# Partial products of a Strassen-like projection stay in SBUF while 13 common tiles are free

## The chip, the cores and the metric

The kernel runs on one NeuronCore of one Trainium2 chip. The metric is the device time of one execution in microseconds (us), given as a median over runs. A difference of less than about 0.3% (5 us) counts here as no difference.

## What is computed

The reference is one layer of a streaming encoder. One input projection of the 1024 x 2048 input feeds two mixers side by side: a sparse attention (group A) and a state-space mixer (group B). Their outputs are joined, projected again and normalised. Cut to what matters here:

```python
u = einsum('bsd,de->bse', h, w_in)               # 1024 x 2048 times 2048 x 6752
q, k, v, z_attn, q_idx, k_idx, w_idx, z_ssd, xbc, dt_raw = split(u)
o_attn = dsa_attention(rope(q), rope(k), v, q_idx, k_idx, w_idx) * silu(z_attn)
o_ssd  = ssd_mixer(xbc, z_ssd, dt_raw, ...)      # conv, chunked scan, gated RMSNorm
sub = einsum('bse,ed->bsd', concat(o_attn, o_ssd), w_out)
out = layer_norm(alpha * h + sub)
```

In the sparse attention an indexer scores the keys of each query and only the 256 best are attended; finding the threshold is a search in many short rounds on VectorE and ScalarE. The change touches only how the input projection holds its intermediate sums.

## The kernel before, in words

**Matmul arithmetic.** All big products are float32-accurate. Each operand is split into a high part (`wh`, `xh`, written by ScalarE) and a rest (`wl`, `xl`, written by VectorE or GpSimd), and three matmuls `wh*xh`, `wh*xl`, `wl*xh` make one product of a 128 x 128 block and a 128 x 512 block. One piece of the stream is a column tile of 128 outputs over 8 such blocks: 24 matmuls into one PSUM bank (`pj`, four of them).

**Two groups of pairs.** Most column tiles of the input projection are taken in pairs (`PLAN`, lines 54 to 62; group 0 has 8 pairs, group 1 has 14). Each pair and both halves of the sequence form a 2 x 2 block product that is made with seven products in place of eight (`product`, line 686). The seven lie in four phases (`ph`), with two products (`f` 0 and 1) in the first three phases and one in the last. The pairs of a group are taken two at a time, a couple: in a phase the order is first pair f=0, second pair f=0, first pair f=1, second pair f=1. Products f=0 and f=1 of a pair share one PSUM bank: f=1 goes on adding to what f=0 left, so that before f=1 starts, another engine must have read the bank (event `ev_after`, waited for in `emit_t`, line 1186).

**Intermediate sums.** In phase 0 `t_save` (line 722) copies the first product of a pair with ScalarE into a tile `x` of tag `u`, writes it to DRAM as `P1`, and frees the tile. In phase 1 `t_ld` (line 756) loads `P1` again, and `t_u` (line 734) adds it to the bank on VectorE: after f=0 that is `U2`, after f=1 `U3`; both are written to DRAM and freed. Phases 2 and 3 load `U3`, `U2` and `U3` once more, and `t_comb` (line 763) adds or subtracts the bank on VectorE to make final columns. So a pair writes three tiles of 128 x 512 float32 (256 KB) and reads four; for 22 pairs that is 66 tiles written. In the profile `P1` is named `p`, and `U2` and `U3` are both named `u`, as the SBUF tiles are.

**What sets the order.** There is no order written by hand. The program keeps a list of tasks (Python generators) and a model of the engines' clocks (`Sim`, line 134). `pump` (line 486) looks through the tasks by priority before each quarter of a piece and issues the first one that `ready` (line 438) passes: its events must be due by the model's clock, no engine that it needs may run ahead of TensorE by more than `SLACK` (2650 ns by the model, line 361), and enough tiles must be free (`avail`, line 395, counts them; `keep` holds some back). The weights of a piece are split (`w_split`, line 944) up to `WAHEAD` = 2 pieces ahead of their use. Each engine then executes its instructions strictly in the order in which they were issued. All data transfers go through one queue, SP's. There are 29 tiles of tag `u` (`NU`, line 30); nearly everything that is not an operand of a matmul lives in them.

All engine instructions are issued through one helper, so the profile puts nearly all of them on line 312, and tile names must be read instead: `pj`, `a` and `o` are PSUM banks, `xr` and `s` raw input tiles and attention scores, `wr` raw weights, `wt` and `t` weights in DRAM, `sm` small vectors of the search for the threshold, `cv` the padded tile that the convolution reads.

Of the kernel before, what the change touches and what calls it, by code (L numbers as in the profile page):

```python
# [27 lines left out]
HIDE = -1.0e30  # L28

NU = 29  # L30
N4 = 8
WAHEAD = 2
SKEEP = 4
# [323 lines left out]
class Flow:  # L357

    SLACK = 2650.0
    MARGIN = 300.0

    def __init__(self, nc):
# [73 lines left out]
    def ready(self, task):  # L438
# [13 lines left out]
        for tag, k in n.slots.items():  # L452
            if self.avail(tag) < k + (min(n.keep, self.spare_u) if tag == "u" else 0):
                return False
        slack = self.SLACK * (0.5 if task.prio >= 6 else 2 if task.prio == 0 else 1)
        return all(self.clk[e] <= self.t + slack for e in (n.eng or ("D" if task.prio >= 6 else "")) if e != "P")
# [126 lines left out]
class Layer:  # L583
    def __init__(self, ctx, tc, a):
# [6 lines left out]
        self.dram = pool("dram", bufs=1, space=bass.MemoryType.DRAM)  # L591
        for tag, n in (("xh", 16), ("xl", 16), ("xr", 2), ("wr", 6), ("wh", 3), ("wl", 3), ("u", NU), ("s4", N4), ("cv", 2), ("sm", 6)):
            fl.add_tag(tag, pool("p_" + tag, bufs=1), n)
# [128 lines left out]
    def t_save(self, gi, c, ps):  # L722

        fl = self.fl
        yield Need("A", u=1)
        x = fl.new("u", [P, HALF])
        fl.act(x, ps)
        fl.signal(self.ev_after(gi, c, 0))
        yield Need("")
        fl.dma(self.p_scr("P1", gi, c), x)  # L730
        fl.free(x)
        fl.signal(self.ev_save["P1", gi, c])

    def t_u(self, gi, c, f, ps):

        fl = self.fl
        name = ("U2", "U3")[f]
        yield Need("V", ev=(self.ev_ld[gi, c, 1, 0],), **({} if f else {"u": 1}))
        y = self.ld[gi, c, 1, 0]
        x = y if f else fl.new("u", [P, HALF])  # L740
        fl.tt("V", x, ps, y, ALU.add)
        if f:
            fl.free(ps)
        else:
            fl.signal(self.ev_after(gi, c, 1))
        yield Need("")
        fl.dma(self.p_scr(name, gi, c), x)
        fl.free(x)
        fl.signal(self.ev_save[name, gi, c])

    def pre_ld(self, gi, c, ph, f):
# [3 lines left out]

    def t_ld(self, name, gi, c, ph, f, e):
        fl = self.fl
        yield Need("", u=1, keep=2, ev=(self.ev_save[name, gi, c],))
        x = self.ld[gi, c, ph, f] = fl.new("u", [P, HALF])
        fl.dma(x, self.p_scr(name, gi, c))  # L760
        fl.signal(e)
# [313 lines left out]
    def run(self):  # L1075
        fl = self.fl
        self.ev_save = {(x, g, c): Event() for x in ("P1", "U2", "U3") for g in range(len(GROUPS)) for c in range(len(GROUPS[g]))}
        self.ev_ld, self.ld, self.wacc, self.xst = {}, {}, set(), {}
        self.stream, work = self.units()
        n = len(self.stream)  # L1080
        self.ev_xs = {k: Event() for k in range(8, 4 * len(self.sets))}
        self.ev_xf = [Event() for _ in range(4)]
        self.xf = {(x, kp): self.scratch(f"xf{x}{kp}", [P, 2, HALF]) for x in ("S1", "M3", "M2", "S4") for kp in range(4)}
        self.wraw, self.w, self.ev_wraw = {}, {}, {}
        self.raws, self.passing = {}, set()
        self.warm_up()
        nf = len(FIRST)
        self.nld = self.start(nf)
        for i, rows in work[2 * nf:]:
            p = self.stream[i]  # L1090
            for q in range(4 if p.kind == "T" else len(rows)):
                fl.pump()
                if q == 0:
                    for f in self.hooks.pop(i, ()):
                        f()
                    while self.nsp < n and self.nsp <= i + WAHEAD + (SKEW if self.late(self.nsp) else 0) and self.w_room() and self.w_there(self.nsp, i):
                        self.w_split(self.nsp)
                        self.nsp += 1
                while self.nld < n and self.nld <= i + WAHEAD + 6 and (self.w_more(self.nld) or self.nld <= i + WAHEAD + 1 and self.w_can(self.nld)):
                    self.w_load(self.nld)  # L1100
                    self.nld += 1
                self.need_w(i)
                if p.kind == "T":
                    self.need_x(("t", p.n, 2 * q), ("t", p.n, 2 * q + 1))
                    self.emit_t(i, q)
                else:
                    if q == 0:
                        self.o_tasks(p.h, p.t, p.u)
                    self.need_x((p.h, 2 * p.u), (p.h, 2 * p.u + 1))
                    self.emit_o(i, p.h, p.t, rows, p.u, q)  # L1110
                    if p.t == 1 and q == len(rows) - 1 and p.h < 6:
                        for k in (2 * p.u, 2 * p.u + 1):
                            fl.free(*self.st.pop((p.h, k)))
            if p.kind == "T" or i < n - SKEW or rows[-1] == 3:
                fl.free(*self.w.pop(i))
                fl.settle(fl.t)
        fl.drain()
# [97 lines left out]
    def o_tasks(self, n, d, j):  # L1215
# [5 lines left out]
        if (n, d, j) == (4, 1, 0):  # L1221
            fl.spare = N4
        if (d, j) == (0, 0) and n < 6:
# [1133 lines left out]
```

## Time and profile before

| what | value |
|---|---|
| median of 3 runs | 1664.8 us (1663.27 to 1667.5) |
| the profiled execution | 1667.98 us |
| its span, first to last instruction | 1666.1 us |
| TensorE (PE) busy | 1620.1 us, 97% of the span |
| VectorE (DVE) busy | 1321.7 us, 79% |
| ScalarE (ACT) busy | 1002.0 us, 60% |
| GpSimd (POOL) busy | 197.3 us, 12% |
| moved by DMA | 414.48 MB, mean 249 GB/s |
| mean granted TensorE clock | 0.992 |

In the profile a row such as `PE pj <- DVE u: 5.6, 4, 4.9` means that TensorE sat idle for 5.6 us in all, 4 times, 4.9 us at the longest, until a VectorE instruction writing a tile `u` released it. A timeline row has the start, the duration, the engine and line, the operation, out<-in, the shapes, the count of merged instructions, and in brackets the idle time of the engine just before and who ended it. A windows row has the stretch, its length, the busy time of PE, PEld (weight loads), DVE, ACT and POOL with the number of instructions, then the granted clock as a share of full speed, the busy share of the DMA engines, and GB/s.

### The profile page before, as it was taken

To read this page: it belongs to the slowest core of one execution; us is meant where nothing else is said; L and a number is where in the kernel's file an instruction comes from. 1 tells how busy PE (TensorE), PEld (TensorE's weight loads), DVE (VectorE), ACT (ScalarE), POOL (GpSimd) and SP (SyncE) were. 2 spreads that over 40 slices of the span, in tenths; PEclk is the share of its full clock that TensorE was granted. 3 is DMA by queue.
4 is the path that set the end of the run, shared out by engine and by line. 5 is a ranking of instruction groups with operands and counts; after the bars stand their busy time and mean duration, and the time that the engine had idled before them with its cause. 6 is when DMAs were issued, how large, how long until landed. Compare 5 with 4: busy or idle time off the path is not lost. (4 is left out here: it accounts for less than half of the span.)

```text
span 1666.1 us, 23979 instructions
## 1 busy us (share of the span) xinstructions
PE 1620.1 (97%) x7996; PEld 1340.9 (80%) x7996; DVE 1321.7 (79%) x2429; ACT 1002.0 (60%) x1770; POOL 197.3 (12%) x215
## 2 busy tenths in 40 slices
PE   9999999999998989999999999999999999999997
PEld 7787777888787768888888888888877888888885
DVE  5889998997778866788676669875787687659998
ACT  4555666779787788776344456776866555532330
POOL 0100010000000000122212202222010000100110
PEclk9999999999999999999999999999999999999999
DMA  8177574789768856687786584656988889668664
GB/s 309 52 280 258 189 262 168 268 303 334 290 230 324 294 196 234 235 304 277 260 288 218 180 286 161 210 171 210 334 284 307 316 300 325 215 232 274 220 202 152
DMA packets 192387, 414.48 MB, mean 249 GB/s; under 512 B 19720, under 2 KB 55688, under 8 KB 192264
## 3 DMA queue, kind: packets, MB, share of 16 engines
q1 hardware_dynamic: 191832, 412.56, 71.7%
q8 instruction: 63, 1.03, 0.2%
q14 instruction: 60, 0.49, 0.1%
q10 hardware_dynamic: 432, 0.39, 0.1%
HBM read 308.94 MB, written 103.94 MB: 248 GB/s over the span
## 5 line engine op out<-in xcount | busy, mean ns | idle before, releaser
L312 PE MATMUL pj<-xh,wh 128*128 128x512 f32 (+1 forms) x1496 | 585.7, 392 | 14.5 <-ACT u L312 6.0
L312 PE MATMUL pj<-xh,wl 128*128 128x512 f32 (+1 forms) x1496 | 573.6, 383 | 5.1 <-DVE wl L312 5.1
L312 PE MATMUL pj<-xl,wh 128*128 128x512 f32 (+1 forms) x1496 | 573.0, 383 | 0.0
L312 DVE TENSOR_TENSOR wl<-wr,wh 128x1024 fp32r<-128x1024 f32 (+2 forms) x236 | 282.4, 1201 | 172.4 <-ACT wh L312 170.4
L312 PEld LDWEIGHTS pj<-xh,wh 128*128 128x128 f32 x1496 | 283.8, 190 | 68.6 <-issue 7.5
L312 PEld LDWEIGHTS pj<-xh,wl 128*128 128x128 f32 x1496 | 283.5, 190 | 63.1 <-DVE wl L312 7.3
L312 PEld LDWEIGHTS pj<-xl,wh 128*128 128x128 f32 x1496 | 284.0, 190 | 49.1
L312 ACT ACTIVATE wh<-wr 128x1024 fp32r<-128x1024 f32 (+2 forms) x242 | 248.1, 1031 | 120.0 <-PE pj L312 82.8
L312 PE MATMUL a<-u,u 128*128 128x512 f32 (+3 forms) x736 | 172.8, 354 | 7.6 <-DVE s L312 4.4
L312 PEld LDWEIGHTS a<-u,u 128*128 128x128 f32 x736 | 120.7, 189 | 42.5 <-DVE s L312 18.6
L312 ACT ACTIVATE u<-a 128x512 fp32r<-128x512 f32 (+4 forms) x115 | 53.2, 479 | 153.3 <-DVE u L312 58.0
L312 ACT ACTIVATE u<-s,sm 128x640 bf16<-128x640 int16 (+7 forms) x132 | 129.7, 983 | 22.1 <-DVE sm L312 20.0
L312 DVE TENSOR_TENSOR u<-u,u 128x512 f32<-128x512 f32 (+6 forms) x204 | 128.6, 645 | 5.7 <-DMA u<-wo 1.3
L312 PE MATMUL pj<-wh,xh 128*128 128x512 f32 x310 | 125.2, 404 | 0.5 <-DVE u L312 0.5
L312 PE MATMUL pj<-wh,xl 128*128 128x512 f32 x310 | 121.0, 390 | 0.0
L312 PE MATMUL pj<-wl,xh 128*128 128x512 f32 x310 | 121.0, 390 | 0.0
L312 ACT ACTIVATE a<-a 128x512 f32<-128x512 f32 (+3 forms) x160 | 77.1, 505 | 68.3 <-PE a L312 65.5
L312 ACT ACTIVATE u<-u 128x512 f32<-128x512 f32 (+4 forms) x146 | 80.1, 558 | 52.4 <-DVE u L312 43.9
L312 DVE TENSOR_TENSOR u<-pj,u 128x512 f32<-128x512 f32 (+2 forms) x112 | 74.7, 668 | 45.7 <-PE pj L312 42.2
L312 DVE TENSOR_TENSOR wr<-wr,wr 128x1024 f32<-128x1024 f32 (+1 forms) x81 | 99.8, 1233 | 0.8 <-DMA wr<-wt 0.4
L312 POOL TENSOR_SCALAR s<-s,sm 128x640 f32<-128x640 f32 (+7 forms) x64 | 63.8, 1011 | 124.0 <-DVE sm L312 97.4
L312 DVE SCALAR_TENSOR_TENSOR u<-cv,cw,u 128x512 f32<-128x512 f32 x96 | 73.0, 766 | 6.7 <-ACT u L312 3.5
(259 smaller groups left out, 2200.3 us busy)
## 6 DMA issues: line engine op xcount, KB each, us to landing
wr<-wt SPq DMA_DIRECT2D x187, 512.0 KB
u<-u SPq DMA_DIRECT2D x110, 256.0 KB
wr<-t SPq DMA_DIRECT2D x44, 512.0 KB
u<-wo SPq DMA_DIRECT2D x64, 256.0 KB
ts<-u SPq DMA_DIRECT2D x64, 256.0 KB
wr<-ts SPq DMA_DIRECT2D x32, 512.0 KB
s<-xt SPq DMA_DIRECT2D x24, 512.0 KB
t<-wr SPq DMA_DIRECT2D x22, 512.0 KB
```

The costliest lines, as they stand in the source:

```text
L312: f(*args, **kw)
```

## The change

Where at least 13 tiles of tag `u` are free at the moment when an intermediate sum is finished, its tile is not freed but kept in a table `kept`. A kept `P1` or `U2` isn't written to DRAM and not loaded; `t_ld` hands the tile on at once. A kept `U3` is still written, since it is needed twice, and only its first load is left out. `t_ld` asks for the save's event first and for a free tile only if it must load. Next to that, `SLACK` goes from 2650 to 2620.

```diff
@@ -28,6 +28,7 @@
 HIDE = -1.0e30
 
 NU = 29
+KEEP_U, KEEP_G = 13, 9
 N4 = 8
 WAHEAD = 2
 SKEEP = 4
@@ -358,7 +359,7 @@
 
 
 
-    SLACK = 2650.0
+    SLACK = 2620.0
     MARGIN = 300.0
 
     def __init__(self, nc):
@@ -727,9 +728,15 @@
         fl.act(x, ps)
         fl.signal(self.ev_after(gi, c, 0))
         yield Need("")
-        fl.dma(self.p_scr("P1", gi, c), x)
-        fl.free(x)
+        if self.may_keep("P1", gi):
+            self.kept["P1", gi, c] = x
+        else:
+            fl.dma(self.p_scr("P1", gi, c), x)
+            fl.free(x)
         fl.signal(self.ev_save["P1", gi, c])
+
+    def may_keep(self, name, gi):
+        return name in ('P1', 'U2', 'U3') and gi < KEEP_G and self.fl.avail("u") >= KEEP_U
 
     def t_u(self, gi, c, f, ps):
 
@@ -744,8 +751,13 @@
         else:
             fl.signal(self.ev_after(gi, c, 1))
         yield Need("")
-        fl.dma(self.p_scr(name, gi, c), x)
-        fl.free(x)
+        stay = self.may_keep(name, gi)
+        if not stay or name == "U3":
+            fl.dma(self.p_scr(name, gi, c), x)
+        if stay:
+            self.kept[name, gi, c] = x
+        else:
+            fl.free(x)
         fl.signal(self.ev_save[name, gi, c])
 
     def pre_ld(self, gi, c, ph, f):
@@ -755,7 +767,12 @@
 
     def t_ld(self, name, gi, c, ph, f, e):
         fl = self.fl
-        yield Need("", u=1, keep=2, ev=(self.ev_save[name, gi, c],))
+        yield Need("", ev=(self.ev_save[name, gi, c],) if (name, gi, c) not in self.kept else ())
+        if (name, gi, c) in self.kept:
+            self.ld[gi, c, ph, f] = self.kept.pop((name, gi, c))
+            fl.signal(e)
+            return
+        yield Need("", u=1, keep=2)
         x = self.ld[gi, c, ph, f] = fl.new("u", [P, HALF])
         fl.dma(x, self.p_scr(name, gi, c))
         fl.signal(e)
@@ -1076,6 +1093,7 @@
         fl = self.fl
         self.ev_save = {(x, g, c): Event() for x in ("P1", "U2", "U3") for g in range(len(GROUPS)) for c in range(len(GROUPS[g]))}
         self.ev_ld, self.ld, self.wacc, self.xst = {}, {}, set(), {}
+        self.kept = {}
         self.stream, work = self.units()
         n = len(self.stream)
         self.ev_xs = {k: Event() for k in range(8, 4 * len(self.sets))}
```

In the built program the condition is met for 10 of the 66 tiles: in group 0 one `P1` (pair 7), four `U2` (pairs 0, 1, 2 and 7) and four `U3` (pairs 1, 5, 6 and 7), in group 1 a single `U3` (pair 8). SP's queue has 1206 DMAs of data where it had 1221, 15 of 256 KB fewer. The matmuls are the same and as many, 7682 instructions in all. ScalarE has 57 table loads in place of 53 and otherwise as many instructions; three sums move from GpSimd to VectorE. The first instruction that is gone is the write of `P1` of pair 7, which stood at 330.99 us in the profile; up to there the orders of all engines are the same, and after it the scheduler takes other decisions on every engine, in the second group and beyond. The last 40 instructions of VectorE, the normalisation, are again the same in kind and order.

Three places show what moved. The first is VectorE in the last phase of group 0, ahead of the split of the weight of pair 3: `wl` is the rest of a weight of the next piece, `wr<-wr,wr` a sum of two raw weights, `cv` and `u<-pj` combine a bank with a loaded or kept sum, `u<-cv,cw` is the convolution. Before (the split of the weight before this one is row 782):

```order
793 L312 SCALAR_TENSOR_TENSOR sm_2975<-sm_2975 128x2
794 L312 TENSOR_TENSOR sm_3784<-sm_3784 128x2
795 L312 TENSOR_SCALAR sm_3784<-sm_3784 128x2
796 L312 SCALAR_TENSOR_TENSOR sm_3784<-sm_3784 128x2
797 L312 SCALAR_TENSOR_TENSOR u_5209<-cv_5356,cw,u_5209 128x512 x3
798 L312 SCALAR_TENSOR_TENSOR u_5094<-cv_5412,cw,u_5094 128x512 x3
799 L312 TENSOR_TENSOR wr_5374<-wr_5374,wr_5375 128x1024
800 L312 TENSOR_TENSOR wl_5432<-wr_5229,wh_5431 128x1024
801 L312 TENSOR_TENSOR wl_5436<-wr_5270,wh_5435 128x1024
```

Now:

```order
790 L313 TENSOR_TENSOR wl_5296<-wr_5093,wh_5295 128x1024
791 L313 TENSOR_TENSOR xl_5320<-xr_5199,xh_5319 128x512
792 L313 TENSOR_TENSOR xl_5324<-s_893_5219,xh_5323 128x512
793 L313 TENSOR_TENSOR xl_5328<-s_893_5219,xh_5327 128x512
794 L313 TENSOR_TENSOR wr_5254<-wr_5254,wr_5255 128x1024
795 L313 TENSOR_TENSOR cv_5347<-pj_5117,u_4333 128x512
796 L313 TENSOR_TENSOR wr_5309<-wr_5309,wr_5310 128x1024
797 L313 TENSOR_TENSOR wl_5351<-wr_5209,wh_5350 128x1024
```

Before, between the two weights (rows 782 and 800) there were two convolutions of three steps each, nine small steps of the search and three sums of weights, and the next weight was split right behind. Now three splits of `x`, two sums of weights and one combination lie between them, and the convolution stands behind the weight.

The second place is ScalarE in phase 0 of group 1, at the second couple (pairs 2 and 3). `u<-pj` is `t_save` of a pair: the bank is free for its second product only when it is done. `u,sm<-` are steps of the search, `wh` is the split of a weight; the table load with the ten instructions on `s` behind it belongs to the state-space mixer. Before:

```order
608 L312 ACTIVATE u_6044<-pj_6006 128x512
609 L312 ACTIVATE u_2976,sm_2975<-s_109_745,sm_2975 128x896
610 L312 ACTIVATE u_2976,sm_2975<-s_110_746,sm_2975 128x1024
611 L312 ACTIVATE wh_6053<-wr_5787 128x1024
612 L312 ACTIVATE u_3785,sm_3784<-u_2425,sm_3784 128x384
613 L312 ACTIVATE u_3785,sm_3784<-u_2426,sm_3784 128x512
614 L312 ACT_TABLE_LOAD
615 L312 ACTIVATE u_5501<-s_953_5496 64x512 x2
616 L312 ACTIVATE s_953_5496<-s_953_5496,ac_241 128x128 x8
617 L312 ACTIVATE u_6107<-pj_6057 128x512
```

Now:

```order
589 L313 ACTIVATE wh_5939<-wr_5668 128x1024
590 L313 ACTIVATE u_5880<-u_5880 128x512
591 L313 ACTIVATE u_2976,sm_2975<-s_109_745,sm_2975 128x896
592 L313 ACTIVATE u_2976,sm_2975<-s_110_746,sm_2975 128x1024
593 L313 ACTIVATE u_5928<-u_5928 128x512
594 L313 ACT_TABLE_LOAD
595 L313 ACTIVATE u_5494<-s_950_5489 64x512 x2
596 L313 ACTIVATE s_950_5489<-s_950_5489,ac_241 128x128 x8
597 L313 ACTIVATE u_5994<-pj_5945 128x512
598 L313 ACTIVATE wh_5998<-wr_5722 128x1024
599 L313 ACTIVATE u_2976,sm_2975<-s_109_745,sm_2975 128x896
600 L313 ACTIVATE u_6035<-pj_6002 128x512
```

Row 608 before was the save of pair 2 and row 617 that of pair 3; now they are rows 597 and 600. The block that begins with the table load stood between the two saves, and stands now ahead of both.

The third place is ScalarE later in phase 0 of group 1, at the couple of pairs 10 and 11, from the split of the weight of pair 11's first product to that of pair 10's second. `s,sm<-s,sm` are exponentials of the attention, `u<-pj` with a table load ahead of it is a SiLU, `u,sm<-u,sm` are steps of the search. Before:

```order
697 L312 ACTIVATE wh_6844<-wr_6557 128x1024
698 L312 ACTIVATE u_3785,sm_3784<-u_2425,sm_3784 128x384
699 L312 ACTIVATE u_3785,sm_3784<-u_2426,sm_3784 128x512
700 L312 ACT_TABLE_LOAD
701 L312 ACTIVATE u_6898<-pj_6694 128x512
702 L312 ACTIVATE u_3785,sm_3784<-u_2425,sm_3784 128x384
703 L312 ACTIVATE u_3785,sm_3784<-u_2426,sm_3784 128x512
704 L312 ACT_TABLE_LOAD
705 L312 ACTIVATE s_1154_6742,sm_6789<-s_1154_6742,sm_6789 128x640
706 L312 ACTIVATE s_1155_6743,sm_6789<-s_1155_6743,sm_6789 128x640
707 L312 ACTIVATE wh_6932<-wr_6576 128x1024
```

Now (the split of the weight before `wh_7013` is row 698, and row 701 is one more table load):

```order
703 L313 ACTIVATE s_1164_6761,sm_6784<-s_1164_6761,sm_6784 128x768
704 L313 ACTIVATE u_3781,sm_3780<-u_2425,sm_3780 128x384
705 L313 ACTIVATE u_3781,sm_3780<-u_2426,sm_3780 128x512
706 L313 ACTIVATE u_6967<-a_6962 128x512
707 L313 ACTIVATE u_3781,sm_3780<-u_2425,sm_3780 128x384
708 L313 ACTIVATE u_3781,sm_3780<-u_2426,sm_3780 128x512
709 L313 ACT_TABLE_LOAD
710 L313 ACTIVATE u_6985<-pj_6684 128x512
711 L313 ACT_TABLE_LOAD
712 L313 ACTIVATE s_1180_6853,sm_6907<-s_1180_6853,sm_6907 128x768
713 L313 ACTIVATE s_1181_6854,sm_6907<-s_1181_6854,sm_6907 128x768
714 L313 ACTIVATE wh_7013<-wr_6577 128x1024
```

Before, the step from one weight to the next had two table loads and two exponentials, in nine instructions between the two splits. Now the step has three table loads and four exponentials, in fifteen: one table load, two exponentials, one pair of search steps and one copy of a bank more.

## The prediction

> **What bounds the kernel now.** I read the busy times first, then the chain that ended last, then who makes TensorE wait, then stretches of the span.
>
> ```profile
> span 1666.1 us, 23979 instructions
> PE 1620.1 (97%) x7996; PEld 1340.9 (80%) x7996; DVE 1321.7 (79%) x2429; ACT 1002.0 (60%) x1770; POOL 197.3 (12%) x215
> 1566.50 21.76 PE pj L312 x96
> ```
>
> TensorE is the bound: 97% of the span, and the last row, from the chain, shows what a dense stretch costs: 96 matmuls in 21.76 us, 0.227 us each, so 5.4 us for a piece of 24. The change removes and adds no matmul. So the time can change only where TensorE idles or runs at a lower clock. These are its longest waits in total:
>
> ```profile
> PE pj L312 <- ACT u L312: 6.0, 2, 4.3
> PE pj L312 <- DVE u L312: 5.6, 4, 4.9
> PE pj L312 <- DVE wl L312: 5.1, 4, 2.6
> PE a L312 <- DVE s L312: 4.4, 7, 2.0
> ```
>
> No row of that answer names a DMA as the releaser of TensorE; the 14 rows name only VectorE, ScalarE and GpSimd. Where do the waits lie? The first two are single events, and stretches of 50 us show the neighbourhood:
>
> ```profile
> 350.00:400.00 50.00, 49.45 (x217) 40.37 (x216) 42.50 (x104) 41.78 (x79) 0.32 (x2) 1.00 0.95 334
> 500.00:550.00 50.00, 43.68 (x186) 35.42 (x186) 43.69 (x78) 38.42 (x71) 3.72 (x7) 0.97 0.85 308
> 550.00:600.00 50.00, 48.27 (x219) 39.37 (x218) 38.63 (x85) 35.90 (x67) 0.80 (x3) 1.00 0.73 260
> 600.00:650.00 50.00, 45.69 (x202) 37.09 (x201) 32.73 (x74) 46.52 (x83) 1.80 (x8) 0.93 0.63 219
> 650.00:700.00 50.00, 50.00 (x229) 41.27 (x227) 38.23 (x89) 37.76 (x70) 3.70 (x4) 1.00 0.77 262
> ```
>
> From 500 to 650 us TensorE is idle for 6.3, 1.7 and 4.3 us. Four waits make nearly all of that:
>
> ```profile
> 519.37 0.77 PE L312 MATMUL pj<-xh,wh 128*128 128x512 f32 x1 [4.89 <-DVE u L312]
> 544.57 0.50 PE L312 MATMUL pj<-xh,wl 128*128 128x512 f32 x1 [1.42 <-DVE wl L312]
> 585.73 0.50 PE L312 MATMUL pj<-xh,wh 128*128 128x512 f32 x1 [1.74 <-ACT u L312]
> 618.56 0.80 PE L312 MATMUL pj<-xh,wh 128*128 128x512 f32 x1 [4.31 <-ACT u L312]
> 519.00:523.00 4.00, 3.63 (x10) 2.96 (x11) 2.67 (x5) 1.32 (x3) 1.23 (x2) 0.60 1.02 388
> 618.00:622.00 4.00, 3.44 (x8) 2.79 (x9) 1.56 (x2) 3.97 (x8) 0.30 (x2) 0.50 0.57 185
> 622.00:626.00 4.00, 4.00 (x14) 3.18 (x13) 3.14 (x4) 3.30 (x7) 0.00 (x0) 0.68 0.68 235
> ```
>
> The three stretches below them show a second price: after the two long waits the granted clock drops. At 0.60 over 4 us TensorE loses 1.6 us, at 0.50 and 0.68 it loses 2.0 and 1.3. So the wait at 519 us costs 6.5 us, that at 618 us 7.6 us.
>
> **The change part by part: the transfers.** Fifteen transfers of 256 KB go, 3.9 MB of 414 MB. What one is to SP's queue:
>
> ```profile
> L312 SPq DMA_DIRECT2D u<-p x22: 320/428/783, 335.7 to 991.5; - x22
> ```
>
> The median issue is 0.43 us, so SP gains about 6 us in all, spread from 331 us to the second group. TensorE waits for no DMA, so I take nothing for them; the cover is that tiles are loaded ahead of their use. The bounds are 0 and, if the stretch at 334 GB/s (the row 350 to 400 above) were bound by transfers, 3.9 MB / 334 GB/s = 11.8 us. That busy row speaks against the upper end: TensorE is busy for 49.45 of its 50 us. The Trainium skill, "DMA: Bandwidth & Descriptors", section Specifications, gives about 358 GB/s as the limit of HBM for one core; by that page the stretch is near its limit, and an estimate from its figure is 11 us of gain. The trace agrees on the rate, and not that the rate binds.
>
> Ten tiles stay held from one phase to the next, out of 29. They are kept only with 13 free, so I take nothing for it; should a task find no tile, it would come later, as part of the next point. `SLACK` is 1% smaller and moves nothing before 331 us.
>
> **The order.** This is what counts: from 331 us the scheduler decides anew. I go through the four waits and put the rows' durations into the new order.
>
> At 544 us TensorE waited for VectorE's split of a weight.
>
> ```profile
> 531.43 1.22 DVE L312 TENSOR_TENSOR wl<-wr,wh 128x1024 fp32r<-128x1024 f32 x1
> 533.17 2.35 DVE L312 TENSOR_TENSOR wr<-wr,wr 128x1024 f32<-128x1024 f32 x2
> 537.68 4.56 DVE L312 SCALAR_TENSOR_TENSOR u<-cv,cw,u 128x512 f32<-128x512 f32 x6
> 542.16 1.22 DVE L312 TENSOR_TENSOR wr<-wr,wr 128x1024 f32<-128x1024 f32 x1
> 543.30 2.35 DVE L312 TENSOR_TENSOR wl<-wr,wh 128x1024 fp32r<-128x1024 f32 x2
> ```
>
> From one split to the next it took 543.30 - 531.43 = 11.9 us, against two pieces of TensorE at 5.4 us. In the new order three splits of `x` at about 0.6 (half of a 1.2 us split, being half as wide), two sums at 1.2, one combination at 0.7 and the split itself make 6.1 us, little more than one piece. The wait goes: -1.4 us. It costs 0 to -1.4.
>
> At 585 us the bank was freed late by ScalarE, by a save that stood behind two steps of the search:
>
> ```profile
> 583.65 0.60 ACT L312 ACTIVATE u<-u,sm 128x384 bf16<-128x384 int16 x1
> 584.38 0.72 ACT L312 ACTIVATE u<-u,sm 128x512 bf16<-128x512 int16 x1
> 585.10 0.57 ACT L312 ACTIVATE u<-pj 128x512 f32<-128x512 f32 x1
> ```
>
> In the new order of ScalarE (rows 571 to 573) the save of pair 0 comes without these two. That is 1.3 of the 1.74 us: -1.3, with bounds 0 and -1.74.
>
> At 519 us the bank of pair 7 waited for a combination on VectorE.
>
> ```profile
> 509.17 1.23 DVE L312 TENSOR_TENSOR wl<-wr,wh 128x1024 fp32r<-128x1024 f32 x1 [4.08 <-ACT wh L312]
> ...
> 518.54 0.68 DVE L312 TENSOR_TENSOR u<-pj,u 128x512 f32<-128x512 f32 x1
> ```
>
> Twelve instructions stand from the first row to the second, 9.4 us. In the new order the tile that this combination adds (`U3` of pair 7) is a kept one, and yet the same twelve, two splits of weights, eight of `x` and two sums, stand ahead of it. So its load was not what made it late, and the wait stays: 0, with bounds of +2 (a part of the 4.08 us idle ahead of it could come twice) and -6.5.
>
> At 618 us ScalarE freed the bank of pair 3 late, after the block of the state-space mixer.
>
> ```profile
> 608.16 1.05 ACT L312 ACTIVATE u<-s,sm 128x896 bf16<-128x896 f32 x1
> 609.33 1.15 ACT L312 ACTIVATE u<-s,sm 128x1024 bf16<-128x1024 f32 x1
> 610.48 1.04 ACT L312 ACTIVATE wh<-wr 128x1024 fp32r<-128x1024 f32 x1
> 612.98 1.28 ACT L312 ACT_TABLE_LOAD   x1
> 615.58 2.44 ACT L312 ACTIVATE s<-s,ac 128x128 f32<-128x128 f32 x8
> 617.93 0.57 ACT L312 ACTIVATE u<-pj 128x512 f32<-128x512 f32 x1
> ```
>
> From the table load to the save it is 617.93 - 612.98 = 4.95 us, about the length of the wait. In the new order this block stands ahead of the save of pair 2, one save earlier. Either pair's second product comes one piece after its first, so the block has the same cover of 5.4 us. I take the wait as moved, not gone: 0, with bounds of +1.9 and -7.6: between the split of the weight and the table load stood 612.98 - 610.48 - 1.04 = 1.5 us, and now stand there the two search steps of the first two rows and two steps of about 0.6, 3.4 us.
>
> **The sum** is -1.4 - 1.3 = -2.7 us against the profiled 1667.98 us, of which the span is 1666.1. Its run lies 3.2 us above the median of the three, so I take the difference over: 1664.8 - 2.7 = 1662.1 us. For the stretches that I didn't go through, mostly behind 650 us, I take nothing: they held few waits before, and may get better or worse. The normalisation at the end is the same.
>
> **The rivals.** *A long wait dissolves.* The waits at 519 and 618 us come from VectorE and ScalarE being late by a few us. For it speaks that VectorE had been idle for 4.08 us just ahead of the twelve instructions, so a split of a weight that ScalarE issues 4 us earlier leaves 0.8 of the 4.89. Against it speaks that the order at both places is nearly the old one. If one goes with its drop of the clock, the time is 1662.1 - 7 = 1655 us; if both go, 1648.
>
> *ScalarE becomes the bound in a step of group 1 (the other side).* At pairs 10 and 11, the step from one weight to the next was:
>
> ```profile
> 696.42 1.05 ACT L312 ACTIVATE wh<-wr 128x1024 fp32r<-128x1024 f32 x1
> 703.57 0.84 ACT L312 ACTIVATE s<-s,sm 128x640 f32<-128x640 f32 x1
> 705.21 1.04 ACT L312 ACTIVATE wh<-wr 128x1024 fp32r<-128x1024 f32 x1
> ```
>
> That is 8.8 us, and TensorE did not wait (650 to 700 us: busy for 50.00). The new step has one table load (1.28), two exponentials (0.84 each at the least), one pair of search steps (0.60 and 0.72) and one copy (0.57) more: 4.9 us, 13.7 in all. If the old step had just no room left, TensorE waits for 4.9 us; as after the 4.31 us at 618 us, 3.3 us of lowered clock would follow. 1662.1 + 8.2 = 1670.3 us. It decides as soon as ScalarE, which splits weights up to two pieces ahead, has less than 4.9 us in hand there; that four table loads came in speaks for it, and that ScalarE is busy for only 37.76 of the 50 us before speaks against it.
>
> *The transfers were the bound after all*: 1664.8 - 11.8 = 1653 us. Speaking for it is the 0.95 share at 350 us; against it, that no DMA releases TensorE. The Trainium skill, "DMA: Bandwidth & Descriptors", section Specifications, has the limit that this case would run into.
>
> *The change hardly does what it says.* It keeps 10 of 66 tiles; if the order is all and evens out, the time is 1664.8. That lies so near the forecast that I count it with it.
>
> **How the numbers follow.** Forecast, with the last case, 0.42: 1662.1, its own range 1660 to 1667. A long wait dissolves, 0.30: 1655 or 1648. ScalarE becomes the bound, 0.22: 1670.3. Transfers, 0.06: 1653. A difference of 0.3%, 5 us, is what a measurement can tell: below 1659.8 is faster, above 1669.8 slower. Faster is 0.30 + 0.06 = 0.36, the same 0.42, slower 0.22. The range reaches from 1652, with one wait gone, to 1672, with 1670.3 and the +1.9 of the fourth wait; beyond it I leave both waits gone (about 0.08) and two overloaded steps (about 0.08).
>
> **What would show it.** In the changed profile: no wait of TensorE for `wl` near 540 us; at the first save of group 1 a wait under 1 us; a wait of 4 to 5 us for VectorE near 515 us, with a clock near 0.6 behind it; a wait of about 4 us for ScalarE's save of pair 2, with the table load ahead. The forecast is wrong if either long wait is missing, if a wait over 3 us appears between 690 and 720 us, or if TensorE's idle time behind 650 us changes by more than 5 us.

## The result

The changed kernel takes 1674.6 us (median of 4 runs, 1673.33 to 1676.72) against 1664.03 us for the kernel before (4 runs, 1662.09 to 1667.5): 1.006 times as long, 95% interval 1.0043 to 1.0077. It is slower by 10.6 us, and the forecast of 1662.1 us, with its range of 1652 to 1672, missed it. One execution each of two kernels below, `plain_2600` (1774.6 us) and `plain_late_2650` (5690.8 us), fell in a slow state and is left out of their times; the only profile of `plain_2600` is of that execution, so only its time is used.

### The profile page after: what moved, and what is told of

Read it like the earlier page. It is cut to its first block, busy times and chain, and to the rows that moved or that the text cites. A ratio compares the mean times of both kernels' runs of the same rounds, so it can differ in the third digit from the quotient of the medians.

```text
span 1673.6 us, 23943 instructions
## 1 busy us (share of the span) xinstructions
PE 1618.2 (97%) x7996; PEld 1340.9 (80%) x7996; DVE 1326.7 (79%) x2432; ACT 1008.9 (60%) x1774; POOL 186.8 (11%) x212
## 5 line engine op out<-in xcount | busy, mean ns | idle before, releaser
L313 PE MATMUL pj<-xh,wh 128*128 128x512 f32 (+1 forms) x1496 | 586.4, 392 | 20.4 <-DVE u L313 12.5
L313 PE MATMUL a<-u,u 128*128 128x512 f32 (+3 forms) x718 | 169.2, 353 | 6.9 <-DVE s L313 3.7
L313 DVE TENSOR_TENSOR u<-u,u 128x512 f32<-128x512 f32 (+6 forms) x210 | 137.6, 666 | 7.3 <-DMA wr<-wt 3.8
L313 PE MATMUL pj<-wh,xh 128*128 128x512 f32 x318 | 129.0, 406 | 1.5 <-DVE xh L313 1.3
L313 POOL TENSOR_SCALAR s<-s,sm 128x640 f32<-128x640 f32 (+7 forms) x64 | 57.3, 908 | 179.1 <-DVE sm L313 159.9
```

What stands on the lines that cost most here:

```text
L313: f(*args, **kw)
```

## The profile after

The head of the changed kernel's page, to be set beside the prediction's first rows:

```profile
span 1673.6 us, 23943 instructions
PE 1618.2 (97%) x7996; PEld 1340.9 (80%) x7996; DVE 1326.7 (79%) x2432; ACT 1008.9 (60%) x1774; POOL 186.8 (11%) x212
```

TensorE is idle for 1673.6 - 1618.2 = 55.4 us, where it was 1666.1 - 1620.1 = 46.0. The idle time grew by 9.4 us and the busy time fell by 1.9, which is the 7.5 us of the span. (The two profiled runs lie 3.95 and 0.85 us above their medians, so the medians differ by 3 us more.) Three stretches show where. Of the kernel before:

```profile
350.00:650.00 300.00, 285.89 (x1254) 232.91 (x1253) 232.11 (x508) 245.96 (x452) 13.98 (x24) 0.98 0.78 278
650.00:1100.00 450.00, 445.81 (x2350) 377.67 (x2349) 346.64 (x697) 265.37 (x495) 95.84 (x96) 1.00 0.71 239
1100.00:1400.00 300.00, 296.72 (x1555) 246.86 (x1554) 222.79 (x384) 193.27 (x329) 37.26 (x41) 0.99 0.84 285
```

and of the changed kernel:

```profile
350.00:650.00 300.00, 283.56 (x1247) 232.06 (x1246) 228.30 (x480) 235.04 (x424) 8.06 (x21) 0.98 0.77 268
650.00:1100.00 450.00, 448.89 (x2385) 382.39 (x2384) 352.49 (x726) 278.82 (x525) 86.39 (x94) 1.00 0.71 240
1100.00:1400.00 300.00, 286.32 (x1499) 235.67 (x1498) 221.47 (x379) 189.47 (x315) 44.58 (x45) 0.99 0.80 273
```

The length less the first busy time is TensorE's idle time: 14.1, 4.2 and 3.3 us before, 16.4, 1.1 and 13.7 us now. The loss is 2.3 us in group 0 and the start of group 1, a gain of 3.1 follows, and then 10.4 us are lost. Most of these fall where no tile is held any more. The last kept tile, a `U3` of pair 8, is added to its bank on VectorE at 1133.57 us; behind 1140 us TensorE idles 3.3 us in the kernel before and 10.4 in the changed one (the two stretches below, in this order), so 7.1 us of the loss lie there and 3.3 us ahead of it.

```profile
1133.57 0.68 DVE L313 TENSOR_TENSOR u<-pj,u 128x512 f32<-128x512 f32 x1
...
1140.00:1400.00 260.00, 256.72 (x1331) 213.01 (x1330) 196.42 (x333) 165.53 (x278) 26.85 (x30) 0.99 0.87 297
...
1140.00:1400.00 260.00, 249.65 (x1307) 205.17 (x1307) 193.44 (x327) 160.18 (x260) 33.95 (x35) 0.99 0.83 284
```

The waits of TensorE, from its timeline: the first four rows lie where the prediction looked, the others are five of the longest between 1100 and 1400 us.

```profile
442.09 0.47 PE L313 MATMUL pj<-xh,wh 128*128 128x512 f32 x1 [2.43 <-DVE u L313]
472.01 0.47 PE L313 MATMUL pj<-xh,wh 128*128 128x512 f32 x1 [1.50 <-DVE u L313]
522.43 0.76 PE L313 MATMUL pj<-xh,wh 128*128 128x512 f32 x1 [6.65 <-DVE u L313]
613.16 0.80 PE L313 MATMUL pj<-xh,wh 128*128 128x512 f32 x1 [5.30 <-ACT u L313]
...
1104.58 0.51 PE L313 MATMUL pj<-xh,wh 128*128 128x512 f32 x1 [1.71 <-DVE u L313]
1133.79 0.63 PE L313 MATMUL a<-c,s 128*128 128x128 f32 x4 [1.61 <-DVE sm L313]
1174.58 0.66 PE L313 MATMUL a<-o,u 128*128 128x1 f32 x4 [1.51 <-POOL u L313]
1284.91 0.70 PE L313 MATMUL a<-u,u 128*128 128x256 f32 x2 [1.28 <-DVE u L313]
1301.59 0.44 PE L313 MATMUL o<-s,u 128*64 128x128 f32 x4 [1.41 <-DVE s L313]
```

The waits of before at 544 and 586 us are gone. Those at 519 and 619 us are still there, at 522 and 613 us, each longer. Those at 442 and 472 us are new. Late in the kernel there is no large wait: many of one to two us, on three engines. How such a small one comes about is seen on VectorE ahead of the wait at 1104 us:

```profile
1099.36 4.57 DVE L313 SCALAR_TENSOR_TENSOR u<-cv,cw,u 128x512 f32<-128x512 f32 x6 [2.55 <-ACT u L313]
1103.84 0.68 DVE L313 TENSOR_TENSOR u<-pj,u 128x512 f32<-128x512 f32 x1
```

VectorE stood idle for 2.55 us until ScalarE had done the first steps of two convolutions, then ran the six steps that follow, and only then the combination (second row) that frees the bank. Nothing was too much here; the combination merely stands behind work that started late.

## The experiments

My theory after the result: the transfers are worth nothing, and the time is set by the order, which the scheduler draws anew on the smallest cause, so that each new order has waits of its own. The rivals: `SLACK` alone makes the loss (1); holding tiles makes it (2); the transfers have a worth that the order hides (3); the late waits are lateness carried over from the front (4). In the table, "idle" is TensorE's in the stretches 350 to 650, 650 to 1100, 1100 to 1400 and 1400 to 1600 us, from windows as above. The kernel before took 1663.8 to 1666.0 us (medians) beside these runs.

| kernel | tiles kept | us | ratio, 95% interval | idle |
|---|---|---|---|---|
| before | 0 | 1664.0 | | 14.1, 4.2, 3.3, 0.2 |
| slack_only | 0 | 1666.4 | 0.9998 to 1.0018 | 8.0, 1.6, 6.6, 4.2 |
| plain_2690 | 0 | 1665.9 | 0.9992 to 1.0014 | 11.6, 8.3, 3.8, 0.2 |
| plain_2600 | 0 | 1678.9 | 1.0063 to 1.0102 | not used |
| before_late_2620 | 0 | 1665.5 | 0.9993 to 1.0022 | 14.9, 4.2, 4.0, 0.2 |
| plain_late_2650 | 0 | 1659.4 | 0.9954 to 0.9976 | 8.4, 1.8, 4.0, 3.9 |
| keep_one | 1 | 1681.8 | 1.0081 to 1.0112 | 15.6, 8.3, 8.1, 0.2 |
| keep_four | 4 | 1674.4 | 1.0037 to 1.0067 | 13.0, 2.5, 8.8, 2.0 |
| after | 10 | 1674.6 | 1.0043 to 1.0077 | 16.4, 1.1, 13.7, 0.2 |
| keep_eighteen | 18 | 1672.3 | 1.0021 to 1.0050 | 8.8, 2.4, 6.1, 7.2 |
| group0_only | 9 | 1709.4 | 1.0240 to 1.0275 | 16.1, 4.7, 13.4, 4.6 |
| keep_only | 9 | 1697.1 | 1.0174 to 1.0206 | 16.9, 6.0, 12.5, 7.4 |
| keep_2600 | 10 | 1679.4 | 1.0068 to 1.0103 | 9.9, 10.3, 12.1, 0.8 |
| keep_2690 | 12 | 1694.1 | 1.0158 to 1.0202 | 16.1, 12.1, 9.9, 0.1 |
| after_late_2650 | 10 | 1681.7 | 1.0076 to 1.0123 | 15.0, 1.2, 11.1, 6.2 |
| after_late_2680 | 10 | 1676.8 | 1.0042 to 1.0082 | 15.1, 3.4, 7.9, 5.3 |
| transfers_back | 10 | 1675.1 | 1.0051 to 1.0079 | 14.9, 1.5, 13.9, 0.2 |
| no_saves | 0 | 1667.2 | 1.0009 to 1.0028 | 16.7, 4.1, 3.6, 0.2 |
| short_search_before | 0 | 1651.9 | 0.9908 to 0.9937 | 7.3, 3.6, 3.6, 0.2 |
| short_search_after | 10 | 1665.5 | 0.9992 to 1.0012 | 12.4, 3.1, 11.8, 0.2 |

**The transfers.** One kernel gives the changed kernel its 15 transfers back in its own order (the loads with 340 of their 512 columns), the other takes the 66 saves from the kernel before in its own order. The second leaves out what the loads should bring, so its output is another one. The code is cut to the lines that count; the save of `P1` is left out in the same way.

```diff
 transfers_back, against the changed kernel (idle_tile is 128 x 340)
+            fl.nc.sync.engine.dma_start(self.p_scr("P1", gi, c), x)
...
+            if name == "U2":
+                fl.nc.sync.engine.dma_start(self.p_scr(name, gi, c), x)
...
+            fl.nc.sync.engine.dma_start(self.idle_tile, self.p_scr(name, gi, c)[:, 0:340])
 no_saves, against the kernel before (no_dma tells only the model)
-        fl.dma(self.p_scr(name, gi, c), x)
+        fl.no_dma(self.p_scr(name, gi, c), x)
...
-        fl.dma(x, self.p_scr(name, gi, c))
+        fl.no_dma(x, self.p_scr(name, gi, c))
+        fl.nc.sync.engine.dma_start(x, self.a["xn"][0:P, 0:HALF])
```

> The changed kernel, every engine's instructions in the same order, but the 15 transfers that it saves are issued again on SP's queue without the scheduler's model hearing of them: the saves whole, each load as 340 of 512 columns into a tile that nobody reads. Theory (transfers hide, only the order counts): 1674.6 us within 3, and the waits at 522, 613 and 1100 to 1400 us stay. Rival 3 (the saved transfers are worth something that the new order hides): slower than the changed kernel, by up to 11.8 us, 1686 us.

> The kernel before in its own order, with all 66 saves of partial products left out and each of the 88 loads taking the same number of bytes from an input instead, so the numbers that come out are others; the scheduler's model is told of the old transfers. 17.3 MB of 414.5 MB go, and no load waits for a save. Theory (transfers hide): 1664 us within 3, with the four waits of before at 519, 545, 586 and 619 us. Rival 3 (transfers bind somewhere): at 334 GB/s 17.3 MB take 52 us, so 1612 us at the far end, and at the least more than 5 us faster, below 1659 us.

With the transfers back the time is 1675.1 us, and the waits at the named places are the changed kernel's to 0.2 us:

```profile
523.38 0.77 PE L313 MATMUL pj<-xh,wh 128*128 128x512 f32 x1 [6.61 <-DVE u L313]
614.56 0.79 PE L313 MATMUL pj<-xh,wh 128*128 128x512 f32 x1 [5.12 <-ACT u L313]
```

and the stretch from 1100 to 1400 us idles 13.9 us, for 13.7:

```profile
1100.00:1400.00 300.00, 286.10 (x1495) 235.01 (x1494) 222.18 (x375) 190.46 (x317) 45.59 (x45) 0.99 0.80 271
```

Only the 1.50 us at 472 us went (the stretch 450 to 500 us idles 0.2 us). Without the 66 saves the kernel before takes 1667.2 us, not less than with them; some waits of its front shift (16.7 us of idle for 14.1), those behind it stay. So 17 MB fewer bring nothing, and rival 3 is out. The Trainium skill, "DMA: Bandwidth & Descriptors", section Specifications, puts the limit of HBM for a core at about 358 GB/s. The prediction had a rival that ran into it, at 334 GB/s; by these two runs no such limit set this kernel's time, and the figure was no ceiling here: `short_search_after`, a kernel further down, moved 391 GB/s on the mean (the last figure of this row), with TensorE busy all the time.

```profile
374.40:416.00 41.60, 41.60 (x185) 34.43 (x185) 34.65 (x76) 23.55 (x64) 0.00 (x0) 1.00 1.02 391
```

**Each half of the change alone**, and both at other values of `SLACK`.

```diff
 slack_only, plain_2600, plain_2690: the kernel before with
-    SLACK = 2650.0
+    SLACK = 2620.0        (2600.0, 2690.0)
 keep_only, keep_2600, keep_2690: the changed kernel with
-    SLACK = 2620.0
+    SLACK = 2650.0        (2600.0, 2690.0)
```

> The kernel before with SLACK 2620 in place of 2650; no tile is kept and no transfer goes. Theory (the scheduler draws the order anew, and the new order's small waits set the time): from about 331 us the order is a third one, with waits of its own; TensorE's idle time can land anywhere from some 36 to 60 us (46.0 before, 55.4 after), so 1655 to 1680 us, and the stretch 1100 to 1400 us need not look like either kernel's. Rival 1 (SLACK alone makes the loss): 1674.6 us within 3, with about 13.7 us of TensorE idle between 1100 and 1400 us. Rival 2 (holding tiles makes the loss): 1664 us within 3, idle there near 3.3 us.

> The changed kernel with SLACK back at 2650; tiles are kept by the same rule. Theory (order drawn anew): again an order of its own, 1655 to 1680 us, not tied to either kernel. Rival 1 (SLACK alone): 1664 us within 3. Rival 2 (holding tiles takes them from other tasks): 1674.6 us within 3, with the loss again between 1100 and 1400 us.

> The changed kernel with SLACK 2600; its order leaves the changed kernel's at about 250 us, before the first tile is kept, so the whole of both groups is drawn anew, with tiles kept by the same rule (17 transfers fewer than in the changed kernel's partner without keeping would need; 1190 rows on SP's queue). Theory (each redraw of the order has its own small waits, whatever is kept): anywhere from 1655 to 1700 us; it need not show waits of about 2.4, 1.5, 6.7 and 5.3 us at 442, 472, 522 and 613 us. Rival 2 (holding tiles itself costs time): slower than 1670 us, with more TensorE idle between 350 and 650 us than the 14.1 us of the kernel before.

> The changed kernel with SLACK 2690; its order leaves the changed kernel's at about 118 us. Theory and rival 2 as for SLACK 2600 with keeping: by the theory anywhere from 1655 to 1700 us, by rival 2 slower than 1670 us with over 14.1 us of TensorE idle between 350 and 650 us.

> The kernel before with SLACK 2600; nothing is kept. Theory (each redraw of the order has its own waits): anywhere from 1655 to 1700 us, and together with SLACK 2690, 2650 (1665.4) and 2620 (1666.4) a spread like that of the four kernels that keep tiles. Rival 2 (holding tiles itself costs time): all four without keeping lie below all four with it, so below 1670 us here.

> The kernel before with SLACK 2690; nothing is kept. Theory: anywhere from 1655 to 1700 us. Rival 2: below 1670 us, and below both kernels of this call that keep tiles.

`SLACK` alone costs nothing (1666.4 us), so rival 1 is out. The new `t_ld` does nothing by itself either: built with a threshold that is never met, the changed program is, instruction for instruction, that of `slack_only`. So what the changed kernel loses against `slack_only`, 8 us, came with the ten kept tiles. But the idle time of `slack_only` is another than before: 6 us less in the front, 7 more behind 1100 us, and the sum came out equal by chance. Keeping alone costs 32 us, three times the loss of the change, and more than I had allowed the theory (1680). It keeps the same nine tiles of group 0 as the changed kernel, and shares its order up to about 579 us, but for two instructions on ScalarE that stand a few places off; the 22 us between the two come from 30 ns of `SLACK` behind that (the one tile of group 1 isn't kept in that order). Two of its waits behind that place:

```profile
1218.21 0.77 PE L313 MATMUL pj<-xh,wh 128*128 128x512 f32 x1 [5.37 <-DVE u L313]
...
1464.90 0.79 PE L313 MATMUL pj<-wh,xh 128*128 128x512 f32 x1 [3.72 <-ACT xh L313]
```

The next four didn't decide between the theory and rival 2. The 1678.9 us of `plain_2600` show that an order with no tile kept can lose 15 us as well, which rival 2 forbade. `keep_2600` is slow, as rival 2 asked, but idles 9.9 us in the front where rival 2 asked for over 14.1. The other two fit both.

**The last part drawn anew**, with the front as it was.

```diff
 in `ready`; self.t is the model's clock, in ns, which there runs ahead of the trace
-        slack = self.SLACK * (0.5 if task.prio >= 6 else 2 if task.prio == 0 else 1)
+        slack = (2620.0 if self.t < 1000e3 else 2650.0) * (0.5 if task.prio >= 6 else 2 if task.prio == 0 else 1)
 after_late_2650: so; after_late_2680: 2620 and 2680
 before_late_2620: the kernel before, 2650 and 2620; plain_late_2650: the kernel before, 2620 and 2650
```

> The changed kernel, SLACK 2620 up to 1000 us of the model's clock and 2650 behind it. Every engine's order is the changed kernel's until about 1190 us of the trace, so the kept tiles and the waits at 442, 472, 522, 613, 1104, 1134 and 1175 us stay; only the last part is drawn anew. Theory (the late loss is a draw of the order, with no tile held any more): the waits behind 1190 us (about 7 us of TensorE idle up to 1400) change, so the time moves by more than 3 us, to 1665 to 1672 or to over 1678 us. Rival 2 (the loss follows from keeping): 1674.6 us within 3.

> The changed kernel, SLACK 2620 up to 1000 us of the model's clock and 2680 behind it. The order is the changed kernel's until about 1055 us. Theory: the 13.7 us of idle between 1100 and 1400 us are another sum, between 3 and 20 us, and the time moves by more than 3 us from 1674.6. Rival 2: 1674.6 us within 3, with 12 to 14 us idle there.

> The kernel before, SLACK 2650 up to 1000 us of the model's clock and 2620 behind it; nothing is kept. The order is that of before until about 1100 us. Theory: the 3.3 us of idle between 1100 and 1400 us become another sum, more often a larger one, up to 14; 1662 to 1685 us. Rival 2: no loss without kept tiles, 1664 us within 3.

> The kernel before with SLACK 2620 up to 1000 us of the model's clock and 2650 behind it; nothing is kept. Up to about 1000 us it is the kernel with SLACK 2620, whose TensorE idles 9.6 us between 350 and 1100 us against 18.3 of before; the last part is drawn anew. Theory: if the last part had the 3.7 us idle of before, 1664 - 9 = 1655 us; as the draw can't be foretold, 1652 to 1680 us. Rival 2: at most 1666 us.

After the changed kernel's front, two other last parts gave 1681.7 and 1676.8 us. (By the traces the four orders leave those that they start from at about 1258, 1078, 1146 and 1267 us, so in all but the second only a part of the stretch from 1100 to 1400 us is new.) The first moved as the theory said. The second moved by only 2.2 us, which by the time alone is rival 2's result, against my "more than 3 us"; its idle time did move, from 13.7 and 0.2 us to 7.9 and 5.3, from one stretch to the next. After the front of before, the new last part changed nothing (idle 4.0 us for 3.3), against my "more often larger". The fourth is faster than both kernels, 0.9965 times the kernel before: its front, that of `slack_only`, has none of the waits of before at 545, 586 and 619 us, and its last part happens to be good:

```profile
350.00:650.00 300.00, 291.59 (x1289) 237.46 (x1288) 239.51 (x516) 250.20 (x456) 12.34 (x24) 0.99 0.82 286
650.00:1100.00 450.00, 448.22 (x2351) 378.94 (x2350) 352.84 (x702) 268.72 (x500) 90.03 (x91) 1.00 0.71 240
1100.00:1400.00 300.00, 296.00 (x1571) 247.06 (x1569) 218.80 (x384) 181.11 (x318) 31.22 (x38) 1.00 0.86 291
```

**The dose.** All kernels with tiles kept were slower so far, so rival 2 was still open.

```diff
-KEEP_U, KEEP_G = 13, 9
+KEEP_U, KEEP_G = 17, 9    keep_one      (15, 9 keep_four; 10, 9 keep_eighteen; 13, 1 group0_only)
```

> The changed kernel with KEEP_U 17, so that only one tile is kept, a U2 of pair 3 in group 0. Up to the first combinations of that pair its order is that of the kernel with SLACK 2620 and nothing kept (1666.4 us). Rival 2 (the loss grows with the tiles kept): 1 tile against 10 that cost 8.2 us over 1666.4, so 1667 us within 3. Theory (a new order, a new draw, however small the cause): anywhere from 1658 to 1697 us, and not tied to the number of tiles.

> The changed kernel with KEEP_U 15: four tiles are kept, all in group 0. Rival 2: 1666.4 + 4 x 0.82 = 1669.7 us within 3. Theory: anywhere from 1658 to 1697 us, with no rule between 1, 4, 10 and 18 tiles.

> The changed kernel with KEEP_U 10: 18 tiles are kept, 13 in group 0 and 5 in group 1, and 13 of the transfers that the changed kernel still makes go. Rival 2: 1666.4 + 18 x 0.82 = 1681 us or more, as the tiles are held out of a shorter supply. Theory: anywhere from 1658 to 1697 us.

> The changed kernel with KEEP_G 1: the same nine tiles of group 0 are kept, and the one of group 1, held from about 900 to 1077 us, is not. Its order is the changed kernel's until about 930 us. Rival 2: one tile less, 1674 us within 3, and the idle time of TensorE between 1100 and 1400 us stays near 13.7. Theory: the last part is another draw; the time moves by more than 3 us, and the waits between 1100 and 1500 us are others.

At the same `SLACK`, 0, 1, 4, 10 and 18 tiles took 1666.4, 1681.8, 1674.4, 1674.6 and 1672.3 us. One tile costs more than eighteen; there is no dose, and rival 2 as I had put it is out. That keeping tiles costs something whatever their number is not excluded: all four lie above the 1666.4 us. Not keeping the one tile of group 1 made the changed kernel 35 us slower, beyond the 1697 us that the theory had allowed the other three; its idle time between 1100 and 1400 us stayed near the changed kernel's (13.4 us for 13.7), as rival 2 had it, but the waits there are others. Its longest waits behind 650 us:

```profile
1219.20 0.76 PE L313 MATMUL pj<-xh,wh 128*128 128x512 f32 x1 [7.14 <-DVE u L313]
...
1610.97 0.79 PE L313 MATMUL pj<-wh,xh 128*128 128x512 f32 x1 [9.46 <-ACT xh L313]
1618.62 0.79 PE L313 MATMUL pj<-wh,xh 128*128 128x512 f32 x1 [6.01 <-ACT xh L313]
```

What releases TensorE at 1610.97 and 1618.62 us is a split of `x` on ScalarE, and in its own rows that one waited for VectorE:

```profile
1610.29 0.63 ACT L313 ACTIVATE xh<-u 128x512 fp32r<-128x512 f32 x1 [7.69 <-DVE u L313]
1617.94 0.63 ACT L313 ACTIVATE xh<-u 128x512 fp32r<-128x512 f32 x1 [7.03 <-DVE u L313]
```

VectorE was doing mostly the final normalisation of finished rows (`mv`) in that time, of which these are two steps; the scheduler had issued them ahead of the input of the next matmul. Here the last kept tile had been used over 1000 us earlier. (The 900 and 1077 us of the expectation are the model's clock; in the trace of the changed kernel that tile is held from 936 to 1134 us.)

```profile
1607.46 0.74 DVE L313 SCALAR_TENSOR_TENSOR u<-u,mv,u 128x512 f32<-128x512 f32 x1
1608.24 0.75 DVE L313 SCALAR_TENSOR_TENSOR u<-u,mv,xh 128x512 f32<-128x512 f32 x1
```

**Is lateness carried on?** In both kernels, each in its own order, the counting steps of the search were cut to 128 columns on the chip, and left as they were in the model. One of the two places that count is shown; the other is cut in the same way.

```diff
-            fl.act(junk[:, 0:n], sc[i][:, 0:n], AF.Sign, bias=cut[:, j:j + 1], accum_out=count[:, j:j + 1])
+            fl.short(junk[:, 0:n], sc[i][:, 0:n], cut[:, j:j + 1], count[:, j:j + 1])
+    def short(self, out, in_, bias, count):
+        self.nc.scalar.engine.activation(out[:, 0:P], in_[:, 0:P], AF.Sign, bias=bias, accum_out=count)
+        self.placed(self.sim.run("A", "activation", [out, count], [in_, bias], {"func": AF.Sign}))
```

> The kernel before, every engine in its own order, but each of the 198 counting steps of the search on ScalarE (173 us in all, between 200 and 800 us, 0.88 us each) reads only 128 columns, so the threshold found is another one; the scheduler's model is told of the full step. Theory (a strict order and an engine that is late at that place make each wait): TensorE's idle time between 350 and 650 us falls from 14.1 to under 9 us, as the waits at 519, 586 and 619 us stand behind such steps; between 1100 and 1400 us it stays at 3.3 within 1.5. 1652 to 1661 us. Rival 4 (lateness is carried on): idle falls everywhere.

> The changed kernel with the same shorter counting steps, in its own order. Theory: idle between 350 and 650 us falls from 16.4 to under 9 us; between 1100 and 1400 us it stays at 13.7 within 2, since no step of the search is left there; the kernel stays 6 to 13 us slower than the kernel before with the same cut. Rival 4 (the waits behind 1100 us are lateness carried over from the front): they fall below 8 us, and the two kernels with the cut come within 4 us of each other.

The two stretches, first of the kernel before with the cut, then of the changed one:

```profile
350.00:650.00 300.00, 292.67 (x1294) 240.00 (x1293) 242.83 (x525) 181.83 (x470) 16.69 (x25) 0.99 0.81 286
1100.00:1400.00 300.00, 296.35 (x1578) 245.98 (x1577) 224.83 (x387) 185.20 (x312) 35.15 (x38) 1.00 0.86 293
```

```profile
350.00:650.00 300.00, 287.55 (x1266) 236.25 (x1265) 232.47 (x492) 174.37 (x436) 7.74 (x19) 0.98 0.76 270
1100.00:1400.00 300.00, 288.19 (x1516) 237.50 (x1514) 218.07 (x376) 193.85 (x325) 43.58 (x44) 1.00 0.82 279
```

Behind 1100 us little moves in either (3.6 us for 3.3, and 11.8 for 13.7, where rival 4 wanted under 8), and the two kernels stay 13.6 us apart, slightly more than the 6 to 13 expected. The changed kernel's waits of 1.71, 1.61 and 1.51 us come again as 1.72, 1.60 and 1.33 us, 8 us earlier. So the waits there belong to the order at that place, and rival 4, tried with the lateness that the search makes, is out. In the front the kernel before loses half its idle time, as expected, and at 1651.9 us it lies at the lower edge of the 1652 to 1661 expected. The changed one keeps 12.4 us, against my "under 9": its waits at 522 and 613 us became 4.93 and 5.68 us, so most of them did not come from the search.

## Why the prediction was wrong

**The step that failed** is "For the stretches that I didn't go through, mostly behind 650 us, I take nothing: they held few waits before, and may get better or worse." It measured +7.1 us of idle time: -3.1 from 650 to 1100, +10.4 from 1100 to 1400, -0.2 behind. "May get better or worse" treats the two sides alike, and they aren't: of 3.3 us at most 3.3 can be gained. In the fourteen kernels of the table that have a new order there, some in a part of it only, and all their work (all but the last four rows, `before` and `plain_2600`), this stretch idles 3.8 to 13.7 us, 8.7 us on the average. Before is better than all of them. Redrawing it was worth +5.4 us on the average, not 0. But the average hides two groups: the four that keep no tile idle 4.6 us there, the ten that keep some 10.4. By those four, a new order alone was worth +1.3 us; why the orders with kept tiles are worse there, mostly with none held any more, no run shows. (The stretch was also picked after the result, because the loss lay there.) The text's own condition, that idle time behind 650 us changes by more than 5 us, is what came true.

**Also left out:** the new waits at 442 and 472 us, 3.9 us together, lie in the front that the prediction did search. It followed the waits of before into the new order and looked for no new ones except at pairs 10 and 11. Between the two profiled runs the forecast of -2.7 us missed by 10.2: 7.1 us from the stretches behind 650 us, 3.9 from the new waits, 2.3 from the four waits below, less 3.1 us of smaller waits and lowered clock that went.

**The four waits.** At 544 and 586 us they went, -1.4 and -1.7 us for -1.4 and -1.3 forecast. At 519 us "the wait stays: 0, with bounds of +2" measured +1.8. The twelve instructions are there as named: from the split of the weight to the combination it is 521.61 - 512.24 = 9.37 us, as before. The reason given for the +2 was another, that VectorE's idle time ahead of them comes twice; it fell from 4.08 to 2.75 us, and the weight came later:

```profile
512.24 1.23 DVE L313 TENSOR_TENSOR wl<-wr,wh 128x1024 fp32r<-128x1024 f32 x1 [2.75 <-ACT wh L313]
...
521.61 0.68 DVE L313 TENSOR_TENSOR u<-pj,u 128x512 f32<-128x512 f32 x1
```

ScalarE does steps of the search straight ahead of the split of that weight, as it did before. From the split ahead of it to this one, these steps between them, it is now 511.17 - 503.55 = 7.6 us; before it was 508.09 - 501.09 = 7.0 us. So 0.6 of the 1.8 us arose in this step, and the rest ahead of it.

```profile
503.55 1.05 ACT L313 ACTIVATE wh<-wr 128x1024 fp32r<-128x1024 f32 x1
...
508.73 0.60 ACT L313 ACTIVATE u<-u,sm 128x384 bf16<-128x384 int16 x1
...
509.32 1.03 ACT L313 ACTIVATE u<-s,sm 128x896 bf16<-128x896 f32 x1
...
510.35 0.82 ACT L313 ACTIVATE u<-s,sm 128x640 bf16<-128x640 f32 x1
...
511.17 1.04 ACT L313 ACTIVATE wh<-wr 128x1024 fp32r<-128x1024 f32 x1
```

and of before:

```profile
501.09 1.04 ACT L312 ACTIVATE wh<-wr 128x1024 fp32r<-128x1024 f32 x1
...
508.09 1.04 ACT L312 ACTIVATE wh<-wr 128x1024 fp32r<-128x1024 f32 x1
```

With the steps of the search cut, VectorE waits 1.57 us in place of 2.75 and TensorE 4.93 in place of 6.65; the rest is the twelve instructions, as the prediction had it. At 618 us "moved, not gone: 0, with bounds of +1.9" measured +1.0, ahead of pair 2, as forecast.

**The rivals.** ScalarE did not become the bound at pairs 10 and 11: from 690 to 720 us no wait exceeds 0.41 us, although the table load and the exponentials moved there. Transfers were not the bound. No long wait dissolved; that they can is shown by `slack_only`, where the one at 619 us is gone with no tile kept.

**What stays open.** The ten kernels that keep tiles took 1672 to 1709 us, the six without 1659 to 1679 (before among them). Five settings of `SLACK` were run both ways, and in none is the kernel with tiles faster: 1679.4 us against 1678.9 (2600), 1674.6 against 1666.4 (2620), 1697.1 against 1664.0 (2650), 1694.1 against 1665.9 (2690), 1681.7 against 1659.4 (2620, then 2650). Several share long parts of their order, so these are not sixteen independent draws. That keeping tiles makes the orders worse as a rule is therefore not excluded, and the table speaks for it; that the order of the changed kernel is a draw like any other is my theory, and not shown. What is shown is that the loss comes with the order and not with the transfers, that the number of tiles doesn't tell it, and that in the changed kernel, `keep_only` and `group0_only` most of it falls where no tile is held.

## What to carry to other kernels

Where a greedy scheduler with a model of the engines writes the program, a small change in a rule is a new order for everything behind it, and its direct saving (here 15 transfers, worth nothing) is small beside the scatter of the orders: here 50 us from settings close to each other. Where the present order has almost no idle time in a stretch, a new one can hardly be better and can be much worse, so count the stretch with a loss, not with zero. How much of the loss belongs to keeping tiles as such stayed open here. Before crediting or blaming such a change, run its neighbours (the threshold one up and one down, the same rule with another margin), and keep the order fixed while the cost in question is taken away or added.

## What the runs showed of the hardware

The granted clock fell behind some short waits and not behind longer ones. Four stretches of the changed kernel: behind 2.43 us of idle, around and behind the 6.65 us (two rows), and behind 1.51 us.

```profile
442.00:446.00 4.00, 3.91 (x19) 3.30 (x20) 3.90 (x13) 1.41 (x3) 0.00 (x0) 1.00 0.59 176
...
519.00:523.00 4.00, 0.57 (x2) 0.50 (x3) 4.00 (x6) 1.10 (x3) 0.00 (x0) 0.58 0.88 316
523.00:527.00 4.00, 4.00 (x12) 3.14 (x11) 2.65 (x5) 2.26 (x4) 1.24 (x2) 0.57 1.04 419
...
1175.00:1179.00 4.00, 4.00 (x17) 3.65 (x17) 0.16 (x1) 0.38 (x1) 3.48 (x3) 0.57 0.17 40
```

After 1.51 us the clock is at 0.57 over 4 us, after 2.43 us at 1.00. The Trainium skill, "TensorE: Matmul & The Clock Gate", Part 1, says that the half rate comes after at least one idle window of about 3.4 us, with windows that run freely. The 6.65 us fit that, the 1.51 us don't; here the measurement decides, and a wait of 1.5 us can cost as much again in lowered clock (4 us at 0.57 lose 1.7 us). What decides between the two cases no run here shows.
